# Moving the modulation sums of a two-layer trunk: new due places, each sum ordered behind a weight split, and a late set-up of the first norm

## The chip, the cores and the metric

One NeuronCore of a Trainium2 chip runs the whole program. The metric is device time in microseconds (us) of one launch. Before the change three runs took 1021.7, 1025.27 and 1025.34 us, a median of 1025.27.

## The reference, cut to what matters

The input is `x` of 256 rows by 1024 columns and a conditioning row `c` of 1024. Two layers have three sub-layers each: a SwiGLU mixer, a sequence mixer, a second SwiGLU mixer. Each sub-layer is modulated by three vectors of 1024 that come from `c`:

```
c_act = silu(c)
for l in range(2):
    mod = c_act @ mod_w[l] + mod_b[l]            # mod_w[l]: 1024 x 9216
    sh1, sc1, g1, sh2, sc2, g2, sh3, sc3, g3 = split(mod, 9)
    f = swiglu(x * (1 + sc1) + sh1, ffn_in[l, 0], ffn_out[l, 0])
    x = layer_norm(ALPHA * x + 0.5 * (1 + g1) * f, ln_g[l, 0], ln_b[l, 0])
    u = x * (1 + sc2) + sh2
    m = even_mixer(u) if l % 2 == 0 else odd_mixer(u)
    x = layer_norm(ALPHA * x + (1 + g2) * m, ...)
    ...                                          # third sub-layer: swiglu with sh3, sc3, g3
```

`swiglu(u) = (silu(u @ w_gate) * (u @ w_up)) @ w_out` with an inner width of 2816. All numbers are float32.

## The kernel before, in words

**Weights as one stream.** The activations stay on the chip with the 1024 columns on the partitions (8 tiles of 128 x 256). All weight matrices are laid out by the host in the order of use, as 170 slabs of 16 blocks of 128 x 128 (1 MiB each, tensor `wst`). `Stream.dma_to` issues the transfers on SyncE's queue (line 331) into the pool `wraw`, which has six buffers. `Stream.conv_to` turns each half slab (8 blocks, 128 x 1024) into two rounded parts: ScalarE writes `whi` (line 351), VectorE writes `wlo = raw - whi` (line 352). That pair is called a split here. `whi` and `wlo` have five buffers each, so splits can run at most five half slabs ahead of TensorE. `mm3` (lines 429 to 431) then makes three matmuls per block: hi by hi, hi by lo, lo by hi. A slab is thus 48 matmuls of 128 x 256. The first slab is used unsplit.

**Modulation sums.** `c_act @ mod_w` isn't done on TensorE. Its matrix is cut into 144 pieces of 128 x 1024; piece i gives the 128 numbers of one eighth of one of the 18 vectors. Two pieces make a 1 MiB transfer (tensor `modw`, line 386, also on SyncE's queue and in the same six `wraw` buffers); there are 72, called mods here, in the order of need: shift and scale of the first sub-layer side by side (mods 0 to 7), its gate (8 to 11), then shift (12 to 15) and scale (16 to 19) of the second, and so on. `Stream.reduce` multiplies a piece by `c_act` and adds along the row in one VectorE instruction (line 403, tile `junk`), then reads the accumulator. This is called a sum here; mod n holds sums 2n and 2n+1.

**What sets the order.** `MOD_TARGETS[s]` says how many mods must have been issued before weight slab s is. `dma_to(s)` first calls `mods_to(MOD_TARGETS[s])`, and a mod remembers the slab in front of which it was issued as its due slab. `conv_to` emits, after the split of a half slab, one sum if the oldest waiting one is due by that slab, and a second one if more than four are waiting. Transfers are issued about four slabs ahead of the split, so several mods wait at a time and sums mostly come out in pairs. `MOD_TARGETS` is made from `FIRST_MODS` (targets of the first slabs), `SHARE` (mods per sub-layer), `SKIP` and `ENDGAP` (slabs left free at a sub-layer's start and end). The first sub-layer is slabs 0 to 32: slabs 0 to 3 for the first half of the inputs and blocks j = 0 to 7 (`W.pause` keeps `conv_to` from emitting sums there), 4 to 11 for j = 8 to 15, 12 to 15 for the second half of j = 0 to 7 (whose earlier part sums lie in the tile `flat`, added at line 811), 16 to 21 for j = 16 to 21, and 22 to 32 for the output matrix. In `first_u` (up to line 567) each of the eight input tiles is modulated as soon as its own two sums are there.

The compiler's framework places the instructions of each engine in one fixed order at build time, from the order of emission, priorities (`tc.high_priority`) and its own picture of when operands are ready. `queue_behind(i, j)` only tells it that i must come after j on their engine. Each engine works through its list in order.

**The norm between sub-layers.** `Boundary(l, s, weight)` is made when the last matrix of a sub-layer begins. Its constructor fetches the gate with `W.mod` (line 583) and scale and shift of the next sub-layer (line 593). `W.mod` forces the transfers and emits all sums still missing for that vector at once. The constructor then makes small 128 x 8 columns `gate`, `A`, `B` and others (lines 585 to 604) and writes `A` and `B` as two extra columns of the tile `flat` (lines 610, 611). `tile_out(f, ps)` takes output tile f out of PSUM with `gate` (line 645) and prepares it for the next sub-layer with `A` (`scaled`, lines 617 and 618); `shift_out` does tile 0.

Of the kernel before, what the change touches and what calls it, by code (L numbers as in the profile page):

```python
# [12 lines left out]
F32R = mybir.dt.float32r  # L13
# [24 lines left out]
SLAB = 16  # L38
# [5 lines left out]
SH, SC, GT = 0, 1, 2  # L44
# [119 lines left out]
SUBS = []  # L164
# [47 lines left out]
def mod_targets():  # L212


    first = FIRST_MODS
    out, done = list(first), first[-1]
    for (a, b), n, skip in zip(SUBS, SHARE, SKIP):
        a, b = max(a // SLAB + skip, len(first)), b // SLAB - ENDGAP
        while len(out) < a:
            out.append(done)  # L220
        out += [done + int(math.ceil(n * (i + 1 - a) / (b - a))) for i in range(a, b)]
        done += n
    out += [NMODSLAB] * (NSLAB - len(out))
    return out


FIRST_MODS = (1, 2, 3, 4, 4, 4, 5, 5, 6, 7, 8, 8)
SHARE = (13, 11, 18, 18, 0, 4)
SKIP = (12, 14, 6, 6, 3, 8)
ENDGAP = 1  # L230
MOD_TARGETS = mod_targets()


@with_exitstack
def trunk_kernel(ctx: ExitStack, tc: tile.TileContext, xT, cvec, pos, wst, modw, colsd,
                 rgw, wa2, outT):
    nc = tc.nc
    sync, act, vec, pool, pe = nc.sync, nc.scalar, nc.vector, nc.gpsimd, nc.tensor
# [10 lines left out]
    wk = ctx.enter_context(tc.tile_pool(name="wk", bufs=2))  # L249
# [10 lines left out]
    def T(pl, shape, dt=F32, tag=None, **kw):  # L260
        return pl.tile(shape, dt, tag=tag, name=nm(tag), **kw)
# [42 lines left out]
    class Stream:  # L304
# [30 lines left out]
        def conv_to(self, n):  # L335

            self.dma_to((n - 1) // 2 + Stream.RAW)
            W2 = Stream.HS * P
            while self.nconv < min(n, 2 * NSLAB):
                s = self.nconv  # L340
                if s < 2 * RAWSLABS:

                    self.conv[s] = (self.raw[s // 2][:, (s % 2) * W2:(s % 2 + 1) * W2], None)
                    if s % 2:
                        self.raw.pop(s // 2)
                    self.nconv += 1
                    continue
                hi = T(whi, [P, W2], F32R, tag="whi")
                lo = T(wlo, [P, W2], F32R, tag="wlo")
                raw = self.raw[s // 2][:, (s % 2) * W2:(s % 2 + 1) * W2]  # L350
                ia = act.activation(hi, raw, AF.Copy)  # L351
                i = vec.tensor_tensor(lo, raw, hi.bitcast(F32), SUB)  # L352
                self.last_conv = ia, i
                if self.behind is not None:
                    queue_behind(i, self.behind)
                self.conv[s] = (hi, lo)
                if s % 2:
                    self.raw.pop(s // 2)
                self.nconv += 1
                if self.todo and not self.pause and self.todo[0][2] <= s // 2:  # L360
                    self.reduce()
                    if len(self.todo) > 4 and self.todo[0][2] <= s // 2:
                        self.reduce()

        def next(self, *keys):
            n = len(keys)
# [53 lines left out]
    W = Stream()  # L420
# [63 lines left out]
    def flat(q, dt=F32):  # L484

        return T(main, [P, KD * FROW], dt, tag=f"flat{q}")
# [88 lines left out]
    class Boundary:  # L575
        def __init__(self, l, s, weight):
            ta.use("abs_reciprocal_sqrt_and_small")
            self.next_table = "silu_and_others" if s != 0 else \
                "natural_log_exp_and_others" if l % 2 == 0 else "abs_reciprocal_sqrt_and_small"
            self.l, self.s, self.weight = l, s, weight  # L580
            self.values = None
            self.done = set()
            g = W.mod(l, 3 * s + GT)
            self.gate = T(wk, [P, KD], tag="gate")
            vec.tensor_scalar(self.gate, g, 1.0, weight, ADD, MULT)
            self.y = T(main, [P, KD, SEQ], tag="yy")
            self.acc = T(wk, [P, 2, SEQ], tag="acc", bufs=1)
            o = (l * 3 + s) * KD
            self.g, self.b = col("ln_g", o, KD), col("ln_b", o, KD)
            self.last = l == DEPTH - 1 and s == 2  # L590
            if not self.last:
                nl, ns = (l, s + 1) if s < 2 else (l + 1, 0)
                sc, sh = W.mod(nl, 3 * ns + SC), W.mod(nl, 3 * ns + SH)
                self.A = T(wk, [P, KD], tag="A")
                self.B = T(wk, [P, KD], tag="B")
                vec.scalar_tensor_tensor(self.A, sc, 1.0, self.g, ADD, MULT)
                vec.scalar_tensor_tensor(self.B, sc, 1.0, self.b, ADD, MULT)
                vec.tensor_tensor(self.B, self.B, sh, ADD)
                self.ag = T(wk, [P, KD], tag="ag")
                self.ab = T(wk, [P, KD], tag="ab")  # L600
                vec.tensor_scalar(self.ag, self.g, -0.5 * ALPHA, None, MULT)
                vec.tensor_scalar(self.ab, self.b, ALPHA, None, MULT)
                self.hA = T(wk, [P, KD], tag="hA")
                vec.tensor_scalar(self.hA, self.A, -0.5, None, MULT)

                self.next = (nl, ns)
                self.ya = [flat(q, F32R)[:, :KD * (SEQ + 2)].rearrange("p (k c) -> p k c", k=KD) for q in range(2)]
                hi, lo = self.ya
                for c, a in ((SEQ, self.A), (SEQ + 1, self.B)):
                    act.activation(hi[:, :, c], a, AF.Copy)  # L610
                    vec.tensor_tensor(lo[:, :, c], a, hi[:, :, c].bitcast(F32), SUB)

        def scaled(self, f):
            if not self.last:
                hi, lo = (t[:, f, :SEQ] for t in self.ya)
                y, a = self.y[:, f, :], self.A[:, f:f + 1]
                act.activation(hi, y, AF.Identity, scale=a)
                vec.scalar_tensor_tensor(lo, y, a, hi.bitcast(F32), MULT, SUB)  # L618
# [21 lines left out]
            self.p0 = (y, ysq)  # L640

        def tile_out(self, f, ps):
            y = self.y[:, f, :]
            with tc.high_priority():
                vec.scalar_tensor_tensor(y, ps, self.gate[:, f:f + 1], ax[:, f, :], MULT, ADD)  # L645
                if f == 0:
                    return
                ysq = T(wk, [P, SEQ], tag="ysq")
                act.activation(ysq, y, AF.Square)  # L649
                if f < KD - 1:  # L650
                    p = self.p0 if f == 1 else (self.acc[:, 0, :], self.acc[:, 1, :])
                    vec.tensor_tensor(self.acc[:, 0, :], p[0], y, ADD)
                    vec.tensor_tensor(self.acc[:, 1, :], p[1], ysq, ADD)  # L653
                self.scaled(f)
            if f == KD - 1:
                self.stats(y, ysq)
# [741 lines left out]
```

## Time and profile before

| what | value |
|---|---|
| median of 3 runs | 1025.27 us (1021.7 to 1025.34) |
| the profiled execution | 1021.95 us, of which the profile's span is 1020.2 us |
| TensorE matmul busy | 997.9 us, 98%, 8344 matmuls |
| VectorE busy | 877.1 us, 86% |
| ScalarE busy | 611.7 us, 60% |
| splits on VectorE (line 352) | 338, 1217 ns each |
| sums on VectorE (line 403) | 136 at 1275 ns and 8 more |
| granted TensorE clock | 0.996 |

PE in the profile is TensorE's matmuls, PEld its weight loads, DVE VectorE, ACT ScalarE, SP SyncE. In a timeline a row is start, duration, engine, line, operation, written tile <- read tiles, shapes; a bracket tells idle time of the engine before it and who ended it. In the rows of waits the numbers are us in total, times, and the longest. In the rows by window an engine's busy time stands with the count of its instructions, then the granted clock, the share of the transfer engines that was busy, and GB/s.

### The profile page before, as it was taken

To read this page: it belongs to the slowest core of one execution; us is meant where nothing else is said; L and a number is where in the kernel's file an instruction comes from. 1 tells how busy PE (TensorE), PEld (TensorE's weight loads), DVE (VectorE), ACT (ScalarE), POOL (GpSimd) and SP (SyncE) were. 2 spreads that over 40 slices of the span, in tenths; PEclk is the share of its full clock that TensorE was granted. 3 is DMA by queue.
4 is the path that set the end of the run, shared out by engine and by line. 5 is a ranking of instruction groups with operands and counts; after the bars stand their busy time and mean duration, and the time that the engine had idled before them with its cause. 6 is when DMAs were issued, how large, how long until landed. Compare 5 with 4: busy or idle time off the path is not lost.

```text
span 1020.2 us, 20536 instructions
## 1 busy us (share of the span) xinstructions
PE 997.9 (98%) x8344; PEld 977.2 (96%) x8344; DVE 877.1 (86%) x1503; ACT 611.7 (60%) x1021; POOL 6.7 (1%) x27
## 2 busy tenths in 40 slices
PE   9999999999999999999999999999999999999995
PEld 7999999998999999999999999999999899999995
DVE  5789999798999899999896899999788799666664
ACT  4756664578895666655545664454568777454542
POOL 0000000000000000000000000000000000000000
PEclk9999999999999999999999999999999999999998
DMA  9997798555468936799986469998743156766501
GB/s 345 416 378 294 284 351 322 218 206 177 155 247 314 351 123 211 280 380 368 358 298 244 160 260 379 328 332 333 282 165 125 48 176 240 266 227 244 191 17 42
DMA packets 38145, 258.56 MB, mean 253 GB/s; under 512 B 4241, under 2 KB 5777, under 8 KB 7714
## 3 DMA queue, kind: packets, MB, share of 16 engines
q1 hardware_dynamic: 38050, 257.25, 67.2%
q8 instruction: 65, 1.06, 0.4%
q14 instruction: 30, 0.25, 0.1%
HBM read 256.18 MB, written 1.05 MB: 252 GB/s over the span
## 4 chain that ended last, share of the span: by engine, by line
PE 84%; DVE 13%; issue 1%; ACT 1%; DVEq 0%; ACTq 0%
PE mm L430 24%; PE mm L429 24%; PE mm L431 24%; DVE wlo L352 4%; DVE junk L403 2%; PE mm L789 2%; PE mm L1068 1%; PE mm L1067 1%; PE mm L1069 1%; DVE yy L645 1%; DVE ax L633 1%; PE ax L789 1%; DVE flat L618 1%; DVE acc L653 0%; DVE flat L811 0%
## 5 line engine op out<-in xcount | busy, mean ns | idle before, releaser
L352 DVE TENSOR_TENSOR wlo<-wraw,whi 128x1024 fp32r<-128x1024 f32 x338 | 409.1, 1217 | 78.5 <-ACT whi L351 77.9
L351 ACT ACTIVATE whi<-wraw 128x1024 fp32r<-128x1024 f32 x338 | 355.4, 1058 | 187.0 <-PE mm L430 150.3
L429 PE MATMUL mm<-uhi,whi 128*128 128x256 f32 x1624 | 448.6, 278 | 2.7 <-ACT uhi L722 1.4
L430 PE MATMUL mm<-ulo,whi 128*128 128x256 f32 x1624 | 449.1, 277 | 0.4 <-DVE ulo L477 0.4
L431 PE MATMUL mm<-uhi,wlo 128*128 128x256 f32 x1624 | 448.8, 277 | 0.0
L429 PEld LDWEIGHTS mm<-uhi,whi 128*128 128x128 f32 x1624 | 304.1, 188 | 3.5 <-ACT uhi L722 1.6
L430 PEld LDWEIGHTS mm<-ulo,whi 128*128 128x128 f32 x1624 | 305.0, 188 | 0.9 <-DVE ulo L477 0.7
L431 PEld LDWEIGHTS mm<-uhi,wlo 128*128 128x128 f32 x1624 | 305.0, 188 | 0.1
L431 PE MATMUL mm<-hhi,wlo 128*128 128x256 f32 x704 | 194.8, 277 | 1.0 <-DVE wlo L352 1.0
L430 PE MATMUL mm<-hlo,whi 128*128 128x256 f32 x704 | 194.7, 277 | 0.0
L429 PE MATMUL mm<-hhi,whi 128*128 128x256 f32 x704 | 194.6, 276 | 0.0
L403 DVE CUSTOM_DVE_ANT_0 junk<-wraw,cact,cols 128x1024 bf16<-128x1024 f32 x136 | 173.3, 1275 | 7.4 <-DMA wraw<-modw 6.3
L431 PEld LDWEIGHTS mm<-hhi,wlo 128*128 128x128 f32 x704 | 132.2, 188 | 1.2 <-DVE wlo L352 1.2
L429 PEld LDWEIGHTS mm<-hhi,whi 128*128 128x128 f32 x704 | 132.2, 188 | 0.0
L430 PEld LDWEIGHTS mm<-hlo,whi 128*128 128x128 f32 x704 | 132.2, 188 | 0.0
L476 ACT ACTIVATE hhi<-h 128x256 fp32r<-128x256 f32 x88 | 35.7, 414 | 60.7 <-DVE h L766 60.5
L649 ACT ACTIVATE ysq<-yy 128x256 f32<-128x256 f32 x42 | 17.3, 414 | 41.9 <-DVE yy L645 39.1
L766 DVE SCALAR_TENSOR_TENSOR h<-mm,sg 128x256 f32<-128x256 f32 x75 | 30.5, 414 | 7.3 <-PE mm L431 7.0
L645 DVE SCALAR_TENSOR_TENSOR yy<-mm,gate,ax 128x256 f32<-128x256 f32 x48 | 23.0, 478 | 15.7 <-PE mm L431 15.7
L477 DVE TENSOR_TENSOR hlo<-h,hhi 128x256 fp32r<-128x256 f32 x88 | 35.6, 413 | 0.2 <-ACT hhi L476 0.2
L451 ACT ACTIVATE sg<-mm 128x256 f32<-128x256 f32 x75 | 27.4, 367 | 8.8 <-PE mm L431 4.9
L429 PE MATMUL mm<-flat,whi 128*128 128x258 f32 x96 | 28.7, 299 | 0.0
(310 smaller groups left out, 1112.1 us busy)
## 6 DMA issues: line engine op xcount, KB each, us to landing
wraw<-wst SPq DMA_DIRECT2D x165, 1024.0 KB, 6.2
wraw<-modw SPq DMA_DIRECT2D x71, 1024.0 KB, 7.2
wraw<-wst SPq DMA_DIRECT2D x10, 512.0 KB, 10.0
wraw<-modw SPq DMA_DIRECT2D x2, 512.0 KB, 5.1
yy<-xT SPq DMA_DIRECT2D x8, 128.0 KB, 10.2
wraw<-rgw SPq DMA_DIRECT2D x1, 1024.0 KB, 4.7
outT<-yy SPq DMA_DIRECT2D x3, 256.0 KB, 2.6
outT<-yy SPq DMA_DIRECT2D x2, 128.0 KB, 2.5
```

The source lines that it names most:

```text
L351: ia = act.activation(hi, raw, AF.Copy)
L352: i = vec.tensor_tensor(lo, raw, hi.bitcast(F32), SUB)
L403: i = vec.tensor_tensor_reduce(junk, t, cact, 1.0, bias, MULT, ADD, self.modcols[(l, v)][:, j:j + 1])
L429: pe.matmul(ps, hi, mh, start=start, stop=False, skip_group_check=shared)
L430: pe.matmul(ps, hi, ml, start=False, stop=False, skip_group_check=shared)
L431: pe.matmul(ps, lo, mh, start=False, stop=stop, skip_group_check=shared)
L451: i = act.activation(out, in_, func, **kw)
L476: act.activation(hi, src, AF.Copy)
L477: return vec.tensor_tensor(lo, src, hi.bitcast(F32), SUB)
L645: vec.scalar_tensor_tensor(y, ps, self.gate[:, f:f + 1], ax[:, f, :], MULT, ADD)
L766: vec.scalar_tensor_tensor(h, pu, bu, sg, ADD, MULT)
L789: pe.matmul(grp[j][:, half * SEQ:(half + 1) * SEQ], wt[w], mv, start=k == ks[0] and half == 0 and t == 0, stop=k == ks[-1] and t == len(te ...
```

## The change

The change has three parts. First, new due places for mods 4 to 20, in the first sub-layer: the targets for slabs 4 to 15 are now 4, 5, 6, 7, 8, 9, 10, 11, 12, 12, 12, 12 (before 4, 4, 5, 5, 6, 7, 8, 8, 9, 10, 10, 11), and the next nine mods go out in front of slabs 16 to 24, one each (before, the next ten were spread over slabs 16 to 30, and the set-up of the first norm asked for one of them early). From slab 30 on the targets are as before. Second, `conv_to` sets `self.after`, so that `reduce` orders each sum that it emits behind the split just emitted, on VectorE. The code does this for every sum that `conv_to` emits, in all sub-layers. Third, the first norm (layer 0, sub-layer 0) makes its gate when output tile 0 is taken out and `A`, `B` and the rest when tile 2 is, and then does `scaled` for tiles 0 and 1. The other norms do all of it in the constructor, through the new function `prepare`.

```
-    for (a, b), n, skip in zip(SUBS, SHARE, SKIP):
-        a, b = max(a // SLAB + skip, len(first)), b // SLAB - ENDGAP
+    for (a, b), n, skip, gap in zip(SUBS, SHARE, SKIP, ENDGAP):
+        a, b = max(a // SLAB + skip, len(first)), b // SLAB - gap
...
-FIRST_MODS = (1, 2, 3, 4, 4, 4, 5, 5, 6, 7, 8, 8)
-SHARE = (13, 11, 18, 18, 0, 4)
-SKIP = (12, 14, 6, 6, 3, 8)
-ENDGAP = 1
+FIRST_MODS = (1, 2, 3, 4, 4, 5, 6, 7, 8, 9, 10, 11, 12, 12, 12, 12)
+SHARE = (9, 11, 18, 18, 0, 4)
+SKIP = (16, 14, 6, 6, 3, 8)
+ENDGAP = (7, 1, 1, 1, 1, 1)
+
+LAZY = 2
...
                 if self.todo and not self.pause and self.todo[0][2] <= s // 2:
+
+                    self.after = i
                     self.reduce()
                     if len(self.todo) > 4 and self.todo[0][2] <= s // 2:
+                        self.after = i
                         self.reduce()
+                    self.after = None
...
-            g = W.mod(l, 3 * s + GT)
-            self.gate = T(wk, [P, KD], tag="gate")
-            vec.tensor_scalar(self.gate, g, 1.0, weight, ADD, MULT)
+            self.gate = None
+            self.lazy = LAZY if (l, s) == (0, 0) else -1
...
+            if self.lazy < 0:
+                self.prepare()
+
+        def prepare(self):
+            l, s = self.l, self.s
+            if self.gate is None:
+                g = W.mod(l, 3 * s + GT)
+                self.gate = T(wk, [P, KD], tag="gate")
+                vec.tensor_scalar(self.gate, g, 1.0, self.weight, ADD, MULT)
+            if self.lazy < 0 and not self.last:
+                nl, ns = self.next
                 sc, sh = W.mod(nl, 3 * ns + SC), W.mod(nl, 3 * ns + SH)
...
         def scaled(self, f):
-            if not self.last:
+            if not self.last and self.lazy < 0:
...
         def tile_out(self, f, ps):
+            if self.lazy >= 0:
+                if f == self.lazy:
+                    self.lazy = -1
+                self.prepare()
+                if self.lazy < 0:
+                    for q in range(f):
+                        self.scaled(q)
```

More of the change, by code (lines that the diff above doesn't have):

```diff
@@ L591, in __init__ @@
             if not self.last:
-                nl, ns = (l, s + 1) if s < 2 else (l + 1, 0)
+                self.next = (l, s + 1) if s < 2 else (l + 1, 0)
+                self.ya = [flat(q, F32R)[:, :KD * (SEQ + 2)].rearrange("p (k c) -> p k c", k=KD) for q in range(2)]
+            if self.lazy < 0:
[8 more added lines that the diff above has]
+                nl, ns = self.next
                 sc, sh = W.mod(nl, 3 * ns + SC), W.mod(nl, 3 * ns + SH)
@@ L604, in __init__ @@
                 vec.tensor_scalar(self.hA, self.A, -0.5, None, MULT)
-                self.next = (nl, ns)
-                self.ya = [flat(q, F32R)[:, :KD * (SEQ + 2)].rearrange("p (k c) -> p k c", k=KD) for q in range(2)]
                 hi, lo = self.ya
```

## The prediction

> **What bounds the kernel now.** I read the page's span and engines first.
>
> ```profile
> span 1020.2 us, 20536 instructions
> PE 997.9 (98%) x8344; PEld 977.2 (96%) x8344; DVE 877.1 (86%) x1503; ACT 611.7 (60%) x1021; POOL 6.7 (1%) x27
> ```
>
> TensorE is the bound: it is busy for 98% of the span. The change takes no matmul away, so it can only remove stretches in which TensorE waits, or add some. So the second view is the list of TensorE's waits, here from 12 us on.
>
> ```profile
> PE ax L1127 <- DVE ut L1129: 1.4, 1, 1.4
> PE mm L429 <- ACT uhi L722: 1.4, 1, 1.4
> PE mm L429 <- ACT sg L451: 1.3, 1, 1.3
> PE ax L1023 <- DVE la L1056: 1.1, 1, 1.1
> PE mm L431 <- DVE wlo L352: 1.0, 1, 1.0
> ```
>
> The change touches two of these, as the windows show: in the first sub-layer TensorE isn't full in 96 to 119 us (1.3 short) and, from the waits, once for a `wlo`.
>
> ```profile
> 40.00:60.00 20.00, 20.00 (x178) 20.00 (x178) 16.51 (x22) 10.44 (x16) 0.00 (x0) 1.00 1.02 415
> 60.00:80.00 20.00, 20.00 (x179) 20.00 (x178) 17.41 (x27) 10.59 (x20) 0.00 (x0) 1.00 0.91 352
> 80.00:96.00 16.00, 16.00 (x143) 15.98 (x142) 15.80 (x25) 9.39 (x14) 0.00 (x0) 1.00 0.68 251
> 96.00:119.00 23.00, 21.69 (x191) 21.49 (x191) 23.00 (x41) 14.19 (x25) 0.00 (x0) 1.00 0.80 302
> 119.00:133.00 14.00, 14.00 (x126) 14.00 (x125) 14.00 (x24) 9.17 (x16) 0.00 (x0) 1.00 0.81 307
> 133.00:160.00 27.00, 27.00 (x240) 27.00 (x240) 27.00 (x54) 15.52 (x20) 0.00 (x0) 1.00 0.93 351
> 160.00:197.00 37.00, 35.98 (x313) 35.59 (x313) 30.97 (x58) 19.44 (x28) 0.86 (x4) 1.00 0.76 285
> ```
>
> Three things stand here. 178 or 179 matmuls run in 20 us (some straddle an edge), so a slab of 48 takes about 5.4 us. VectorE (the fifth number) has 3.5 and 2.6 us to spare in 40 to 80, nothing from 96 to 160, and 6.0 us afterwards. The transfer engines (the last share) are full to beyond 60 us.
>
> Now the first stall, in VectorE's timeline and then in ScalarE's and TensorE's.
>
> ```profile
> 113.97 1.21 DVE L352 TENSOR_TENSOR wlo<-wraw,whi 128x1024 fp32r<-128x1024 f32 x1
> 115.11 1.27 DVE L403 CUSTOM_DVE_ANT_0 junk<-wraw,cact,cols 128x1024 bf16<-128x1024 f32 x1
> 116.31 0.07 DVE L403 DVE_READ_ACCUMULATOR2_ANT mod<- 128x1 f32 x1
> 116.31 0.41 DVE L477 TENSOR_TENSOR hlo<-h,hhi 128x256 fp32r<-128x256 f32 x1
> 116.65 0.67 DVE L811 TENSOR_TENSOR flat<-ax,flat 128x512 f32<-128x512 f32 x1
> 117.25 1.26 DVE L403 CUSTOM_DVE_ANT_0 junk<-wraw,cact,cols 128x1024 bf16<-128x1024 f32 x1
> 118.45 0.07 DVE L403 DVE_READ_ACCUMULATOR2_ANT mod<- 128x1 f32 x1
> 118.45 0.41 DVE L766 SCALAR_TENSOR_TENSOR h<-flat,sg 128x256 f32<-128x256 f32 x1
> 118.79 0.41 DVE L766 SCALAR_TENSOR_TENSOR h<-mm,sg 128x256 f32<-128x256 f32 x1
> 119.12 1.20 DVE L352 TENSOR_TENSOR wlo<-wraw,whi 128x1024 fp32r<-128x1024 f32 x1
> ```
>
> ```profile
> 117.42 0.42 ACT L451 ACTIVATE sg<-flat 128x256 f32<-128x256 f32 x1 [1.97 <-DVE flat L811]
> ```
>
> ```profile
> 118.16 0.39 PE L429 MATMUL mm<-uhi,whi 128*128 128x256 f32 x1 [1.31 <-ACT sg L451]
> ```
>
> TensorE needs a PSUM buffer back at 116.85. Its reader `sg` stands on ScalarE behind an `sg` that waited 1.97 us for the add at 116.65, and that add stood behind the sum at 115.11. From start to start a split costs VectorE 1.14 us, a sum about 1.2, an `hlo` or `h` 0.34, an add 0.60. The last split of the fence came after two sums of one mod (115.11 and 117.25). The second stall is in the output matrix.
>
> ```profile
> 157.32 1.21 DVE L352 TENSOR_TENSOR wlo<-wraw,whi 128x1024 fp32r<-128x1024 f32 x1
> 158.46 0.15 DVE L860 TENSOR_SCALAR rg_sp<-rg_sp 128x8 f32<-128x8 f32 x1
> 158.53 1.27 DVE L403 CUSTOM_DVE_ANT_0 junk<-wraw,cact,cols 128x1024 bf16<-128x1024 f32 x1
> ...
> 162.10 1.22 DVE L352 TENSOR_TENSOR wlo<-wraw,whi 128x1024 fp32r<-128x1024 f32 x1
> ```
>
> ```profile
> 163.38 0.39 PE L431 MATMUL mm<-hhi,wlo 128*128 128x256 f32 x1 [1.02 <-DVE wlo L352]
> ```
>
> The split at 162.10 comes late, behind the sums of mods 16 to 19. The constructor of the first norm emits these eight in one go, since they weren't due yet.
>
> **The change part by part.** The work itself stays: 144 sums, 338 splits, the same transfers, the same small columns. Only order and place move, so the terms are stalls that go and stalls that come. All due places below are worked out from the code's plan.
>
> *Slabs 4 to 15 (35 to 100 us).* Four more mods must pass by slab 12 (12 instead of 8). VectorE then has, per slab with a mod, two splits, two sums and for the last four input tiles one `ulo` (about an `hlo`): 2 x 1.14 + 2 x 1.2 + 0.34 = 5.0 us against 5.4 of TensorE. That fits, using the 6.1 us that 40 to 80 leaves free. The queue of transfers: a slab and a mod are 2.1 MB, at 415 GB/s 5.05 us, plus 0.3 us for an input tile of 0.13 MB, which is 5.4 of 5.4. It is full, but keeps pace. I put this at 0. Bounds: nothing below, since no matmul waits in 40 to 96 us now; above, a wait like the longest ones in the list, 1.4 us, twice.
>
> *Slabs 16 to 24 (100 to 150 us).* Up to 133 us the groups of VectorE's instructions from 96 us on say:
>
> ```profile
> L352 DVE TENSOR_TENSOR wlo<-wraw,whi 128x1024 fp32r<-128x1024 f32 x14 | 16.9, 1206 | 0.0
> L403 DVE CUSTOM_DVE_ANT_0 junk<-wraw,cact,cols 128x1024 bf16<-128x1024 f32 x8 | 10.2, 1270 | 0.0
> ```
>
> By the plan the sums of mods 8 to 11 are due three slabs (16 us) earlier than now and slabs 13 to 15 bring none, so I expect VectorE to reach 96 us about two splits and two sums ahead (2.3 + 2.4 = 4.7 us). The product steps of j = 0 to 7 (8 adds, 16 `h` and `hlo`: 4.8 + 5.4 = 10.2 us) and j = 16 (0.34) then share the engine with splits of slabs 17 and 18 (4 x 1.14 = 4.6) and sums 26 to 29 (4.8): 20 us, to 116.0. Before, the last of these steps began at 118.79. The 1.3 us stall asks for 1.3 us sooner; 2.8 are there. It goes: -1.3. Bounds: -1.3 and, if more sums are taken in between, the slower rival below.
>
> *The first norm.* Its columns cost the same as before. Mods 12 to 19 are now due by slab 23 at the latest and need no burst at slab 22, so no eight sums are emitted ahead of the splits; `A` is needed only at tile 2, some 22 us after the output matrix begins at about 133 us. What hides the columns and the late `scaled` of two tiles (0.4 us each on VectorE, by the 128x256 forms above) is VectorE's free 6.0 us in 160 to 197; without that cover they would cost 0.8 us. The stall of 1.0 goes: -1.0. Bounds -1.0 and 0.
>
> *All later sums.* The order behind a split holds for them too. The first sums of the second sub-layer move furthest, from an idle spot to behind a split 26 us later:
>
> ```profile
> 250.21 1.28 DVE L403 CUSTOM_DVE_ANT_0 junk<-wraw,cact,cols 128x1024 bf16<-128x1024 f32 x1 [0.64 <-DMA wraw<-modw]
> ...
> 276.60 1.21 DVE L352 TENSOR_TENSOR wlo<-wraw,whi 128x1024 fp32r<-128x1024 f32 x1
> ...
> 351.79 1.23 DVE L352 TENSOR_TENSOR wlo<-wraw,whi 128x1024 fp32r<-128x1024 f32 x1 [1.81 <-ACT whi L351]
> 353.94 2.36 DVE L352 TENSOR_TENSOR wlo<-wraw,whi 128x1024 fp32r<-128x1024 f32 x2 [0.92 <-ACT whi L351]
> ```
>
> Two sums are 2.4 to 2.6 us in a stretch where `la` holds TensorE up by 1.1 us already. They can push later work by at most 2.6; the idle 1.81 + 0.92 = 2.7 us near 352 take that up again before the transposes at L1127. I take 0, the end nearest those rows; bounds 0 and 2.6. What waits behind a sum that waits for its split: the next split on VectorE, and on SyncE's queue the transfer that reuses the sum's `wraw` buffer. In the later SwiGLU layers a split runs up to five half slabs (13 us) ahead of its use, so I price that at 0 as well.
>
> Sum: -1.3 - 1.0 = -2.3 us. The profiled execution took 1021.95 us (span 1020.2 and 1.75 around it) and would take 1019.65. The median of the three runs is 3.3 us above that execution. The forecast goes by the median: 1025.27 - 2.3 = 1023.0.
>
> **The rivals.**
>
> *It doesn't do what it says (0.30).* The condition for a second sum (more than four waiting) stays, and the plan gives pairs for nearly all of mods 4 to 18: "one by one" isn't what the code does. Pairs behind splits may hold the add just as now, and the stall at 118 us stays while only the one at 163 goes: -1.0, so 1024.3. For it: the pair in the fence was emitted after its splits already. Against it: VectorE's lead of 4.7 us.
>
> *Slower: VectorE falls behind in slabs 17 to 23 (0.13).* Due places put sums 26 to 39 behind splits up to slab 23, which are made before TensorE reaches 133 us. VectorE is full there now with 8 sums in 96 to 133; the lead covers sums up to 33. If the fixed order takes sums 34 to 39 ahead of the splits and product steps, 6 x 1.27 = 7.6 us come on top, and TensorE waits for `wlo` or PSUM. With the 1.0 saved later that is +6.6: 1031.9. It decides from the point where a split of slabs 20 to 23 ends after TensorE has come to it.
>
> *The transfers bind (0.06).* If the queue loses pace while mods 4 to 11 ride one per slab, every slab waits. The rows show 415 GB/s held in 40 to 60. At the 352 of 60 to 80 (where its share is down to 0.91) 2.1 MB take 6.0 us: 0.6 too many for seven slabs, +4.2, less 2.3: 1027.2. The Trainium skill, in "DMA: Bandwidth & Descriptors", section "Where 436 GB/s comes from", says that for transfers from HBM the HBM side, about 358 GB/s, binds. By that rule this rival's number is about what would come; the 415 GB/s of this trace speak against the rule here.
>
> *More goes than I count (0.08).* If the shifted sums also free `la`, `ut` and `uhi`, all five stalls of the list go: 6.2 us, 1019.1; from the fastest run, 1021.7, 1015.5. Against it: these three waits are in the second sub-layer and behind its norm, where targets don't move.
>
> **How the numbers follow.** The forecast has 0.43. About 0.5% (5.1 us) is what a measurement of this kernel can tell from no change. Forecast, first rival, most of the transfers rival and a part of the last lie within it: 0.80. Slower by more: the second rival at most of its price and the far end of the third, 0.13. Faster by more: only the last rival together with the spread of runs, 0.07. The range takes in the full price of the slower rival half way and the runs' own spread of 3.6 us below the median: from 1023.0 down to 1018.0 (-2.3 from the fastest run is 1019.4, and part of the last rival), up to 1030.5.
>
> **What would show it.** Right: in the waits of TensorE the rows for `sg` and for `wlo` are gone, windows 96 to 119 and 160 to 197 show PE full up to the norm, VectorE has idle time already before 160 us, and transfers stay full to about 72 us. The step on slabs 16 to 24 is wrong if TensorE still waits there for `sg`, or newly for `wlo`. The step on later sums is wrong if new waits stand between 270 and 400 us. The forecast as a whole is wrong if the median leaves 1018 to 1030.5.

## The result, and the profile after

| | runs | median, us | lowest to highest |
|---|---|---|---|
| before | 6 | 1022.51 | 1021.7 to 1025.34 |
| after | 6 | 1032.32 | 1030.94 to 1035.64 |

The ratio is 1.0102, with a 95% interval of 1.0088 to 1.0115. The change makes the kernel 9.8 us slower, and the median lies above the range of the prediction. The profiled execution took 1035.32 us, one of the longer of the six.

First the page's span and engines, for the kernel after.

```profile
span 1033.6 us, 20527 instructions
PE 1005.1 (97%) x8344; PEld 981.4 (95%) x8344; DVE 878.6 (85%) x1503; ACT 614.8 (59%) x1021; POOL 6.7 (1%) x27
```

The same 8344 matmuls, and the work of VectorE and ScalarE is the same to 0.5%. So the 13.4 us of span are not work: by the slab starts below some 9.7 are waits, and about 3.4 come with two stretches of half clock (last section). TensorE's waits from 12 us on, the longest:

```profile
PE ax L1149 <- DVE ut L1151: 3.0, 1, 3.0
PE mm L437 <- DVE wlo L354: 3.0, 6, 1.0
PE mm L435 <- ACT whi L353: 2.0, 3, 0.9
PE mm L435 <- ACT uhi L744: 1.4, 1, 1.4
...
PE ax L643 <- ACT shift L641: 0.6, 1, 0.6
...
PE mm L435 <- ACT sg L457: 0.2, 1, 0.2
```

The wait for `sg` has shrunk to 0.2 as forecast. In its place stand three waits for `whi`, which means ScalarE, an engine that the prediction never priced; six for `wlo`; and the wait at the transposes (L1149, which was L1127) has gone from 1.4 to 3.0. The windows show where:

```profile
40.00:60.00 20.00, 18.87 (x162) 18.43 (x161) 14.94 (x21) 9.59 (x14) 0.00 (x0) 1.00 0.97 382
60.00:80.00 20.00, 19.09 (x164) 18.73 (x163) 16.54 (x24) 7.78 (x11) 0.00 (x0) 1.00 0.86 334
80.00:96.00 16.00, 14.44 (x114) 13.33 (x114) 16.00 (x28) 12.23 (x22) 0.00 (x0) 1.00 0.85 311
96.00:119.00 23.00, 23.00 (x205) 23.00 (x205) 23.00 (x39) 13.16 (x21) 0.00 (x0) 1.00 0.86 313
119.00:133.00 14.00, 12.77 (x109) 12.38 (x109) 14.00 (x25) 7.49 (x15) 0.00 (x0) 1.00 0.76 295
133.00:160.00 27.00, 26.17 (x227) 25.77 (x227) 25.50 (x43) 16.36 (x21) 0.00 (x0) 1.00 0.93 355
160.00:197.00 37.00, 36.37 (x321) 36.18 (x320) 30.34 (x63) 18.76 (x27) 0.00 (x0) 1.00 0.66 242
```

Read the counts here, not the busy times. In 40 to 96 us TensorE ran 162 + 164 + 114 = 440 matmuls, before 178 + 179 + 143 = 500. Sixty matmuls at 20 / 178.5 = 0.112 us are 6.7 us. The busy times show a lack of only 3.6: in the timeline a matmul's row lasts 0.28 us although the rows start 0.11 us apart, so the row ahead of a wait covers its first part, and the matmul behind a wait is drawn longer (0.39). The rows of waits are too short for the same reason. So two thirds of the loss lie in the stretch that the prediction called free, and 96 to 119 us is full, as it said.

To follow the loss through the program and through all kernels, I took from each trace the start of a slab's first weight load and subtracted the same in before. Where a stretch of half TensorE clock (last section) lies ahead of the slab, half its length is taken out. In before, slab 4 starts at 34.8 us, 9 at 62.1, 16 at 100.3, 21 at 129.1, 25 at 151.0, 26 at 156.4, 28 at 168.6, 54 at 335.6, 59 at 367.9 and 140 at 846.3. The lags in us, for after and for the experiments below:

| kernel | 4 | 9 | 16 | 21 | 25 | 26 | 28 | 54 | 59 | 140 |
|---|---|---|---|---|---|---|---|---|---|---|
| after | 0.5 | 3.8 | 7.2 | 7.8 | 8.9 | 9.8 | 8.5 | 8.4 | 9.7 | 9.7 |
| places alone | -0.7 | 4.4 | 6.1 | 5.6 | 6.0 | 8.6 | 7.4 | 7.4 | 7.5 | 7.5 |
| order alone | 0.0 | 0.0 | 0.0 | 2.1 | 2.1 | 4.0 | 2.8 | 2.7 | 3.9 | 3.8 |
| set-up alone | 0.2 | 0.2 | 0.2 | 0.2 | 1.5 | 1.5 | 0.2 | 0.2 | -0.3 | 0.0 |
| no order | 0.1 | 5.2 | 6.9 | 6.4 | 6.9 | 7.2 | 5.9 | 5.8 | 5.9 | 6.0 |
| old early places | 0.5 | 0.5 | 0.5 | 5.5 | 7.8 | 7.8 | 6.5 | 6.3 | 7.7 | 7.7 |
| modulation held back | 0.1 | 1.4 | 1.9 | 2.4 | 3.8 | 3.8 | 2.5 | 2.6 | 2.5 | 2.5 |
| before, held back | 1.2 | 1.2 | 1.2 | 1.2 | 1.2 | 1.2 | 1.3 | 1.2 | 1.1 | 1.2 |
| single sums | 0.0 | 3.4 | 6.8 | 6.5 | 6.5 | 7.9 | 6.7 | 6.9 | 8.4 | 8.9 |
| no order, held back | 0.3 | 0.3 | 0.8 | 0.1 | 0.2 | 0.2 | -1.1 | -1.2 | -1.2 | -1.2 |
| set-up, gate early | -0.5 | -0.5 | -0.5 | -0.5 | -0.5 | -0.5 | -1.8 | -1.8 | -1.8 | -1.5 |
| late places, held back | -0.6 | -0.6 | -0.6 | 2.0 | 2.5 | 3.7 | 2.4 | 2.4 | 2.4 | 2.5 |
| order in the first sub-layer | -0.1 | 3.4 | 6.8 | 7.3 | 7.6 | 7.8 | 6.5 | 6.5 | 6.5 | 6.4 |
| no order, held back, gate early | 0.1 | 0.3 | 0.8 | 0.1 | 0.2 | 0.2 | -1.1 | -1.2 | -1.2 | -1.2 |

Only differences along a row count (the first column is the start). In after 6.7 us come between slabs 4 and 16, 1.3 net between 16 and 28 (2.6 up to slab 26, less the 1.3 of before's wait at 163 us, which is gone), and 1.3 between 54 and 59. After slab 59 nothing moves until the end.

The first 6.7 us are to be seen on ScalarE. First its waits in 35 to 96 us of after, then, in 35 to 80 us, of before.

```profile
ACT uhi L560 <- DVE mod L409: 14.3, 4, 3.9
```

```profile
ACT uhi L554 <- DVE mod L403: 13.3, 4, 4.1
```

Four times, once for each of the input tiles 4 to 7, ScalarE stands for some 3.5 us in front of the modulation of a tile (`uhi`, then `ut`), which needs both sums of that tile's mod. Before has this wait too. What differs is what is queued behind it. ScalarE's timeline, after and then before:

```profile
43.13 0.60 ACT L560 ACTIVATE uhi<-yy,mod,mod 128x256 fp32r<-128x256 f32 x1 [3.25 <-DVE mod L409]
...
44.13 1.99 ACT L353 ACTIVATE whi<-wraw 128x1024 fp32r<-128x1024 f32 x2
...
50.02 0.60 ACT L560 ACTIVATE uhi<-yy,mod,mod 128x256 fp32r<-128x256 f32 x1 [3.59 <-DVE mod L409]
...
51.02 1.99 ACT L353 ACTIVATE whi<-wraw 128x1024 fp32r<-128x1024 f32 x2
...
57.90 1.99 ACT L353 ACTIVATE whi<-wraw 128x1024 fp32r<-128x1024 f32 x2
...
64.78 1.99 ACT L353 ACTIVATE whi<-wraw 128x1024 fp32r<-128x1024 f32 x2
```

```profile
42.47 0.60 ACT L554 ACTIVATE uhi<-yy,mod,mod 128x256 fp32r<-128x256 f32 x1 [1.75 <-DVE mod L403]
...
43.47 2.00 ACT L351 ACTIVATE whi<-wraw 128x1024 fp32r<-128x1024 f32 x2
...
50.88 2.00 ACT L351 ACTIVATE whi<-wraw 128x1024 fp32r<-128x1024 f32 x2
```

The clock times are nearly the same; the slab isn't. Counted from the first split, the `whi` at 44.13 in after are those of slab 6, the `whi` at 43.47 in before those of slab 7. With the slab starts of TensorE beside them (of the same traces), the lead being the time from the first `whi` to TensorE's start of the slab:

| tile | before: slab, `whi` starts, TensorE at the slab | lead | after: slab, `whi`, TensorE | lead |
|---|---|---|---|---|
| 4 | 7: 43.47, 51.17 | 7.7 | 6: 44.13, 46.21 | 2.1 |
| 5 | 8: 50.88, 56.61 | 5.7 | 7: 51.02, 52.11 | 1.1 |
| 6 | 9: 57.89, 62.05 | 4.2 | 8: 57.90, 58.99 | 1.1 |
| 7 | 10: 64.90, 67.49 | 2.6 | 9: 64.78, 65.87 | 1.1 |

Each step is one round. In after it is both `whi` of a slab, the first `wlo`, a sum, the second `wlo`, a sum, `uhi`, then the next slab's `whi`; in before both sums stand behind the second `wlo`. In after a round takes 6.88 us (44.13, 51.02, 57.90, 64.78), in before 7.0 to 7.4, against 5.44 us in which TensorE uses a slab up. Each round thus loses 1.4 to 2 us of lead. Before enters with 7.7 and comes out with 2.6. After enters with 2.1 and is down to 1.1 a round later, which is no lead: one `whi` takes about 1.05 us, and TensorE starts the slab as it ends, so that the next two slabs take TensorE 6.88 us each as well. Neither VectorE nor ScalarE is full in this loop (14.9 and 9.6 of the 20 us from 40 on).

The rounds themselves cost 3.3 of the 6.7 us (up to slab 9). The rest follows by slab 14: VectorE did 31.5 us of work from 40 to 80, in before 33.9, though more sums were due. From 80 to 96 it is full with what is left, and TensorE waits for `wlo` and `h`.

The Trainium skill, in "PSUM — Partial Sum Buffer", section "Engine vs sequencer instructions", says that the queues of ScalarE and VectorE are strictly first in, first out; the trace agrees, with each `whi` of the fence for after starting right behind a `uhi` and `ut` that had waited 3.25 to 3.89 us.

### The profile page after: what moved, and what is told of

The parts are those of the page before. It is cut to its first block, busy times and chain, and to the rows that moved or that the text cites. A ratio compares the mean times of both kernels' runs of the same rounds, so it can differ in the third digit from the quotient of the medians.

```text
span 1033.6 us, 20527 instructions
## 1 busy us (share of the span) xinstructions
PE 1005.1 (97%) x8344; PEld 981.4 (95%) x8344; DVE 878.6 (85%) x1503; ACT 614.8 (59%) x1021; POOL 6.7 (1%) x27
## 3 DMA queue, kind: packets, MB, share of 16 engines
HBM read 256.18 MB, written 1.05 MB: 249 GB/s over the span
## 4 chain that ended last, share of the span: by engine, by line
PE 80%; DVE 14%; issue 3%; ACT 2%; DMA 1%; SPq 0%; DVEq 0%; ACTq 0%
PE mm L436 23%; PE mm L437 23%; PE mm L435 23%; DVE wlo L354 5%; DVE junk L409 3%; PE mm L811 2%; ACT whi L353 1%; PE mm L1089 1%; PE mm L1090 1%; PE mm L1091 1%; DMA wraw<-wst 1%; DVE h L788 1%; PE ax L811 1%; DVE hlo L483 1%; DVE flat L633 0%
## 5 line engine op out<-in xcount | busy, mean ns | idle before, releaser
L483 DVE TENSOR_TENSOR hlo<-h,hhi 128x256 fp32r<-128x256 f32 x88 | 36.9, 427 | 0.5 <-ACT hhi L482 0.5
```

The lines of the kernel that those rows point to most:

```text
L483: return vec.tensor_tensor(lo, src, hi.bitcast(F32), SUB)
```

## The experiments

**The three parts alone.** Before with the new places (`FIRST_MODS`, `SHARE`, `SKIP`, `ENDGAP`) and nothing else:

```
-FIRST_MODS = (1, 2, 3, 4, 4, 4, 5, 5, 6, 7, 8, 8)
+FIRST_MODS = (1, 2, 3, 4, 4, 5, 6, 7, 8, 9, 10, 11, 12, 12, 12, 12)
...
```

> The kernel before with the new due places alone. Theory 1 (the places cost, through ScalarE's order): in this build the modulation of input tile 4, which waits for both sums of mod 4, stands on ScalarE in front of the splits of slab 5, where it stands in front of slab 7 in the kernel before and of slab 6 in the changed one. The round of sums, modulation, split takes about 6.9 us per slab against 5.4 of TensorE, so the lead is used up sooner: at slab 16 TensorE is 7 us or more behind the kernel before, in all +7 to +11 us. Theory 2 (the order behind the splits costs): without that order the time stays within 2 us of the kernel before. Theory 3 (transfers bind): about +4 us, with ScalarE's splits waiting for weights rather than for sums.

Measured: 1030.74 us against 1022.3, ratio 1.0081 (1.0066 to 1.0096). This part alone makes most of the loss, 6.8 us of it before slab 16. In this kernel the modulation of tile 4 stands in front of slab 5's split, one slab earlier than in after. TensorE's waits in 35 to 200 us are two rows, and both are waits for splits:

```profile
PE mm L429 <- ACT whi L351: 4.1, 5, 1.2
PE mm L431 <- DVE wlo L352: 3.5, 3, 2.5
```

Before with the order behind the splits alone:

```
+                    self.after = i
                     self.reduce()
                     if len(self.todo) > 4 and self.todo[0][2] <= s // 2:
+                        self.after = i
                         self.reduce()
+                    self.after = None
```

> The kernel before with only the order of each sum behind its split. Theory 1: the modulation of input tile 4 stands in front of slab 8 or 7 as before, so slabs 5 to 16 lose nothing: within 2 us of the kernel before, plus up to 1.5 us of a longer wait before the transposes in the second sub-layer. Theory 2: most of the loss is here, +7 to +10 us. Theory 3: within 2 us.

Measured: 1028.33 us, ratio 1.0054 (1.0037 to 1.0071). The 6.0 us lie between theory 1 (3.5 at most) and theory 2 (7 to 10). Nothing is lost up to slab 16, as theory 1 said; then 4.0 us by slab 26, which it didn't have, and 1.2 at slabs 54 to 59. TensorE's timeline has these waits up to 122 us, and a third of 1.68 us for a `wlo` at 158.21:

```profile
115.89 0.39 PE L435 MATMUL mm<-uhi,wlo 128*128 128x256 f32 x1 [1.04 <-DVE wlo L352]
120.28 0.39 PE L433 MATMUL mm<-uhi,whi 128*128 128x256 f32 x1 [1.61 <-ACT sg L455]
```

The second is before's wait for `sg`, at the same place and longer: there was 1.3. So the order makes the stall that the change was expected to remove a little worse. It also holds sums back into the product steps: the last sum of the gate begins at 100.36 us, in before at 94.98.

Before with the late set-up of the first norm alone:

> The kernel before with only the late set-up of the first norm. All theories: the one wait for wlo in the output matrix (1.0 us) may go: between -1.5 and +0.5 us.

Measured: 1022.66 us, ratio 1.0001 (0.9991 to 1.0011). The lags show two things that cancel: 1.3 us lost by slab 25, and 1.3 gained by slab 28, where before waited for a `wlo`. The loss, in VectorE's timeline:

```profile
147.20 0.17 DVE L604 TENSOR_SCALAR gate<-mod 128x8 f32<-128x8 f32 x1
147.27 1.22 DVE L354 TENSOR_TENSOR wlo<-wraw,whi 128x1024 fp32r<-128x1024 f32 x1
148.41 0.48 DVE L663 SCALAR_TENSOR_TENSOR yy<-mm,gate,ax 128x256 f32<-128x256 f32 x1
```

The first output tile is taken out at 148.41, in before at 143.34, because the gate stands 9 us later on VectorE. The rows of before:

```profile
138.25 0.15 DVE L585 TENSOR_SCALAR gate<-mod 128x8 f32<-128x8 f32 x1
...
143.34 0.48 DVE L645 SCALAR_TENSOR_TENSOR yy<-mm,gate,ax 128x256 f32<-128x256 f32 x1
```

ScalarE's `shift` reads that tile, and a matmul waits 1.0 us for it. The three parts alone cost 8.4, 6.0 and 0.4 us, together 9.8. They don't add up, so each is also taken away from after.

**Taking one part away.** After without the order:

```
-                    self.after = i
                     self.reduce()
...
```

> The changed kernel without the order behind the splits (new places and late set-up stay). Theory 1: like the new places alone, +6 to +11 us against the kernel before. Theory 2: the loss goes, within 2 us of the kernel before or faster. Theory 3: about +4 us.

Measured: 1028.3 us, ratio 1.0056 (1.0041 to 1.0071). The early loss stays (6.8), the later ones go: slabs 16 to 28 gain 1.0, and at slab 59 nothing happens. In this kernel too the modulation of tile 4 stands one slab earlier still, in front of slab 5's split (38.64 us).

After with before's places for slabs 4 to 15 (ten mods left for slabs 16 to 24):

```
-FIRST_MODS = (1, 2, 3, 4, 4, 5, 6, 7, 8, 9, 10, 11, 12, 12, 12, 12)
-SHARE = (9, 11, 18, 18, 0, 4)
+FIRST_MODS = (1, 2, 3, 4, 4, 4, 5, 5, 6, 7, 8, 8, 9, 10, 10, 11)
+SHARE = (10, 11, 18, 18, 0, 4)
```

> The changed kernel with the due places of slabs 0 to 15 as in the kernel before (11 mods by slab 15); slabs 16 to 24 bring the next ten, order and late set-up stay. Theory 1: the early round begins where it did before, so slabs 5 to 16 lose nothing and what is left of the loss is at most 3 us (slabs 24 to 26 and the wait before the transposes). Theory 2: the loss of 10 us stays. Theory 3: most of the loss goes, as in theory 1, but the waits for weights in slabs 16 to 24 grow.

Measured: 1029.98 us against 1022.29, ratio 1.0073 (1.0056 to 1.0090). Before slab 16 nothing is lost now: the early places are the cause of the 6.7 us. But 7.2 us appear between slabs 16 and 25, so that 7.7 are left where theory 1 allowed 3. About 2.0 of them stand at slab 25, where a matmul waits 1.7 us for `shift`; the gate is made at 153.03 here. The new early places do take load off VectorE, as the prediction said; the price is paid earlier.

**Is it ScalarE's queue?** After with the modulation of tiles 4 to 7 ordered on ScalarE behind the first `whi` of the slab four further on (slab 8 for tile 4), that is, about two slabs later. The sums, splits and transfers keep their order:

```
                 self.last_conv = ia, i
+                self.acts[s] = ia
...
             on_act.append(act.activation(uhi[:, k, :], x0[:, k, :], AF.Identity, bias=sh0[:, kk], scale=scp0[:, kk]))
+            if not stepwise:
+                queue_behind(on_act[-1], W.acts[2 * k + 8])
...
         on_act.append(act.activation(ut, x0[:, k, :], AF.Identity, bias=sh0[:, kk], scale=scp0[:, kk]))
+        if not stepwise:
+            queue_behind(on_act[-1], on_act[-2])
```

> The changed kernel; the modulation of input tiles 4 to 7 is ordered on ScalarE behind the first split of the slab that uses it (tile k behind slab k+4), so no split waits for sums there. Theory 1: the 6.9 us round is cut; slabs 5 to 12 run at 5.4 us and 4 to 7 of the 10 us go. If instead VectorE or the buffers of raw weights set the pace, less than 2 us go.

Measured: 1028.57 us, ratio 1.0059 (1.0044 to 1.0074). Of the 6.7 us up to slab 16 only 1.8 are left. By the medians 3.5 of the 9.8 us go, less than the 4 to 7 expected; by the spans of the two profiled executions (1033.6 and 1026.2) it is 7.4. The medians mix in stretches of half clock (last section). The windows to 96 us:

```profile
40.00:60.00 20.00, 18.97 (x167) 18.77 (x166) 18.66 (x26) 10.30 (x14) 0.00 (x0) 1.00 1.02 418
60.00:80.00 20.00, 20.00 (x179) 20.00 (x178) 18.22 (x29) 11.33 (x20) 0.00 (x0) 1.00 1.01 419
80.00:96.00 16.00, 15.96 (x138) 15.63 (x137) 15.48 (x24) 10.13 (x18) 0.00 (x0) 1.00 0.79 300
```

484 matmuls instead of 440. VectorE does more in 40 to 80 than in after (36.9 us instead of 31.5), with the same sums, because its splits no longer wait for a ScalarE that waits for its sums. Most of what is left, 1.3 of the 1.8 us, is one wait in 40 to 60 that the edit brings itself: tile 4 comes late for slab 8.

```profile
58.85 0.39 PE L438 MATMUL mm<-ulo,whi 128*128 128x256 f32 x1 [1.03 <-DVE ulo L572]
```

The same edit in before:

> The kernel before with the same order for the modulation of input tiles 4 to 7. Theory 1: its lead at slab 10 is larger, TensorE had no wait there, so the time changes only by what the later backlog of VectorE gains: between -2 and 0 us. If the place of the modulation itself is critical, it is slower by 1 to 3 us.

Measured: 1022.17 us, ratio 1.0000 (0.9991 to 1.0010). So holding the modulation back is no gain in itself; it only undoes what the new places did.

Both together, after without the order and with the modulation held back:

> The changed kernel without the order behind the splits, and with the modulation of input tiles 4 to 7 behind the first split of the slab that uses it. Two separate causes are claimed: the places through ScalarE's order in slabs 5 to 16 (6.8 us, of which this order gave back 4.8), and the order behind splits in slabs 16 to 28 and before the transposes (2 to 5 us and 1.3 us). If they are separate and these two edits undo them, the time is within 2 us of the kernel before: 1021 to 1024.5. If the places cost by the transfers or the buffers of raw weights as well, it stays at 1026 or above.

Measured: 1021.14 us against 1022.43, ratio 0.9989 (0.9980 to 0.9998). The new places now cost 0.5 us to slab 16:

```profile
40.00:60.00 20.00, 20.00 (x179) 20.00 (x178) 19.46 (x26) 10.39 (x14) 0.00 (x0) 1.00 1.02 417
60.00:80.00 20.00, 20.00 (x179) 20.00 (x179) 17.73 (x29) 11.29 (x19) 0.00 (x0) 1.00 1.01 421
80.00:96.00 16.00, 15.88 (x138) 15.57 (x137) 15.96 (x24) 10.15 (x18) 0.00 (x0) 1.00 0.92 360
```

It also settles the transfers: the same ones run at 417 and 421 GB/s for 40 us with TensorE full. The 382 and 334 of after are not their limit; SyncE's queue waits there 39 of the 40 us for VectorE to free a buffer.

**Is it the pairs?** After with pairs of sums only if more than twelve wait:

```
-                    if len(self.todo) > 4 and self.todo[0][2] <= s // 2:
+                    if len(self.todo) > 12 and self.todo[0][2] <= s // 2:
```

> The changed kernel with one sum at most behind a split (the second one is never emitted in practice). Theory 1: ScalarE's order is the same, so the early loss stays: within 2 us of the changed kernel. Rival: the pairs are what delays the splits; then 4 us or more of the 10 go.

Measured: 1033.78 us, ratio 1.0111 (1.0095 to 1.0126). Nothing changes up to slab 16 (6.8 lost), but nothing could: VectorE's instructions stand in the same order in both kernels up to 110 us, because in after the sums come one by one there already, each behind its own split. So this run can't tell what pairs cost early. The kernel without the order can: its sums come in pairs there, and it loses the same 6.8. Behind slab 16 single sums lose 1.4 us less to slab 28 and 0.7 more from 54 to 140. My first rival, that the code keeps its pairs, is true of the code but, up to slab 16, not of the engine.

**The gate.** Set-up alone as above, but with the gate made in the constructor and only `A`, `B` at tile 2:

> The kernel before with A and B of the first norm made at their first use, but the gate in the constructor, as before. Theory: late set-up alone gained nothing since the late gate holds tile 0 and its shift matmul (1.0 to 1.3 us wait) where a wait for wlo went (1.0 us). With the early gate both are gone: 1.0 to 1.5 us faster than the kernel before. Rival: the wait for wlo had moved for another reason; then no difference.

Measured: 1021.03 us against 1022.43, ratio 0.9987 (0.9978 to 0.9996). The loss at slab 25 is gone and the gain at slab 28 stays: 1.3 us. The gate stands at 137.75 here, and tile 0 is taken out at 142.73. The two changes of the set-up must be told apart: late `A`, `B` gain, a late gate loses as much.

**Late places.** No order, modulation held back, gate early, but before's places to slab 15 and ten mods in slabs 16 to 24:

> The places of slabs 0 to 15 as before, the next ten mods in front of slabs 16 to 24, no order behind splits, A and B late with an early gate, the modulation of tiles 4 to 7 behind the first split of the slab that uses it. Theory: no early round, no late order; what is left are the waits at slab 19 (1.3 us) and in the output matrix, and the places there take sums out of the output matrix: 0 to 2.5 us faster than the kernel before. Rival (more sums in slabs 16 to 24 overload VectorE there by themselves): 1 to 4 us slower.

Measured: 1025.15 us against 1022.43, ratio 1.0026 (1.0015 to 1.0037); 4.3 us lost between slabs 16 and 26 with no order at all: the rival was right. So ten mods in that stretch cost even without the order. Nine mods there cost nothing net where the new early places had taken sums away before (no order, held back: 0.8 at slab 16, 0.2 at slab 26).

**The transposes.** After with the order for the first sub-layer's sums only:

```
-                    self.after = i
+                    self.after = i if s < 66 else None
...
```

> The changed kernel with the order behind splits for the sums of the first sub-layer alone. Theory: the 1.3 us before the transposes of the second sub-layer come from the order of its own sums: 1 to 1.5 us of the 10 go, the rest stays. Rival: they come from the first sub-layer being late; then nothing goes.

Measured: 1029.03 us against 1022.43, ratio 1.0063 (1.0050 to 1.0077). Slabs 54 to 59 lose nothing, and TensorE's wait is back at before's size:

```profile
PE ax L1149 <- DVE ut L1151: 1.4, 1, 1.4
```

In after VectorE's timeline at this place reads

```profile
361.49 0.17 DVE L614 SCALAR_TENSOR_TENSOR A<-mod,cols 128x8 f32<-128x8 f32 x1
...
366.71 1.23 DVE L354 TENSOR_TENSOR wlo<-wraw,whi 128x1024 fp32r<-128x1024 f32 x1 [1.90 <-ACT whi L353]
367.85 0.87 DVE L1151 SCALAR_TENSOR_TENSOR ut<-ax,cols,yy 128x256 f32<-128x256 f32 x2
```

and in before

```profile
347.93 0.15 DVE L596 SCALAR_TENSOR_TENSOR A<-mod,cols 128x8 f32<-128x8 f32 x1
```

The `ut` for which TensorE waits 3.0 us stands behind a split that waits 1.90 us for its `whi`; before has such a wait too (1.81). What is later is the head of the chain, the column `A` of this norm, which needs the last sums. ScalarE's next instruction waits for it (3.06 us in before), and the `whi` come behind that. In before `A` is made at 347.93; with the lag of 8.4 and 1.7 for the clock that would be 358.0 in after, and it is 361.49, because each of the last sums stands behind a split. The idle time that I had counted as a reserve comes after `A` on the chain, so it moves along instead of taking anything up.

**Both gains at once.** No order, modulation held back, and the gate in the constructor:

> This kernel keeps the new places, sets no order behind splits, holds ScalarE's modulation of tiles 4 to 7 behind the first split of the slab four further on, and makes the gate of the first norm in its constructor (A and B at tile 2). Theory: the places cost nothing once the modulation no longer stands in front of the next splits, and the late gate is the only part of the set-up that costs; the two gains (0.9989 for the kernel with the late gate, and 1.3 us at slabs 26 to 28 where the gate came first with the old places) are in different stretches and add up: 0.9976, 2.4 us below before, with no TensorE wait for wlo or shift between 119 and 165 us. Rival: with the new places the late gate costs nothing, since VectorE has time there; then it equals 0.9989, 1.1 us below before, and the wait for the shift is absent in both or present in both.

Measured: 1021.54 us against 1022.13, ratio 0.9993 (0.9984 to 1.0002). The two gains don't add up: the early gate adds nothing here, and the lags are those of the kernel with the late gate. The rival forecast that, but not for its reason. VectorE's timeline says why. With the gate written in the constructor the row is

```profile
75.74 0.16 DVE L609 TENSOR_SCALAR gate<-mod 128x8 f32<-128x8 f32 x1
```

and with the gate written at its first use

```profile
75.74 0.16 DVE L610 TENSOR_SCALAR gate<-mod 128x8 f32<-128x8 f32 x1
```

It stands at the same time in both, 68 us ahead of its use. The instructions of TensorE, VectorE and ScalarE stand in the same order in both kernels from start to end, so this run doesn't test the gate; 0.9989 and 0.9993 are two measurements of one order. In after the gate is made at 98.60. The program's builder can thus place it far ahead of where the code emits it, and "made at its first use" is then not what happens on the engine. What decides the place isn't shown: early sums alone don't, for with the modulation held back and the order kept the last sum of the gate begins at 83.26 (in after 88.92) and the gate stands at 151.21.

## Why the prediction was wrong

**The step that failed: "Slabs 4 to 15 ... I put this at 0".** It measured 6.7 us. (All in all the miss is 12.1 us: against the 1022.51 of six runs the forecast of -2.3 means 1020.2. The 1025.27 of three runs was a high base.) I counted VectorE (5.0 us a slab) and the transfers (5.4) against TensorE's 5.4, each for itself, and both counts held: after the modulation is held back and the order taken off, the same sums and transfers run beside a TensorE that loses 0.5 us. What I left out is that the sums have a reader on ScalarE, `uhi`, and that ScalarE works in a fixed order with splits behind it. Moving the sums of mods 4 to 7 one or two slabs earlier moved `uhi` one slab earlier in that order, in front of a split with 2.1 us of lead instead of 7.7, and that is one round's loss away from waiting. The clue was in the trace of before: four waits of ScalarE for `mod`, 13.3 us in all, which harm nobody there. I looked only at TensorE's waits. My upper bound, "a wait like the longest ones in the list, 1.4 us, twice", priced a single wait, not a loop that comes round four times. How the loss divides is shown: 4.9 us go with the place of `uhi` alone. Of the other 1.8, 1.3 are the wait for `ulo` of tile 4 that the held-back modulation brings, and it goes when the order goes too (0.5 is left). With before's early places the order costs nothing there.

**"Slabs 16 to 24": -1.3.** Half right. The wait for `sg` is down to 0.2 and 96 to 119 us is full. But new waits stand right behind, mostly for `wlo`: 1.2 us are missing in 119 to 133, 0.8 in 133 to 160. "Newly for `wlo`" was this step's own sign of being wrong. By the slab starts after gains 1.1 at slab 19 and then loses 3.7 up to slab 26. Without the order, with the same places, 1.6 are gained and 1.8 lost, so about half of the new waits come from the order and the rest from the places. Part of them is another queue, the wait of 0.6 for `shift`. ScalarE's timeline of after:

```profile
153.57 1.06 ACT L353 ACTIVATE whi<-wraw 128x1024 fp32r<-128x1024 f32 x1 [4.37 <-DMA wraw<-wst]
154.54 0.40 ACT L641 ACTIVATE shift<-yy 128x256 fp32r<-128x256 f32 x1
```

The `shift` stands behind a split that waits 4.37 us for its weights, which are needed later than it.

**"The first norm": -1.0.** The wait at 163 us is gone, worth 1.3. The prediction put it down to the eight sums; between the two splits at 157.32 and 162.10 stand one sum and about 2.4 us of `A`, `B`, the output tile and other small work. In the kernel with before's places the late gate took the same 1.3 back, a term that I didn't have. I asked what hides the late columns, not who reads the gate. In after the gate isn't late at all.

**"All later sums": 0, bounds 0 and 2.6.** It measured 1.3 in slabs 54 to 59, with the wait for `ut` up from 1.4 to 3.0. I let the idle 2.7 us near 352 absorb it; that idle time stands behind the late column on the very chain that TensorE waits for.

**The rivals.** The slower one, 1031.9, comes within 0.5 us of the result for the wrong reason: it put 7.6 us into slabs 17 to 23, where 0.8 net were lost. Its mechanism exists, as the kernel with before's early places shows (5.2 us from slab 16 to 23), but after had moved that load away. The transfers don't bind. By the Trainium skill, "DMA: Bandwidth & Descriptors", section "Where 436 GB/s comes from", the HBM side would hold them at about 358 GB/s, which the section works out as half of what a stack gives two cores. This program runs on one core, and its windows with 417 and 421 GB/s disagree. Pairs instead of single sums change nothing up to slab 16.

**What was right:** no work is added, the -1.3 and the -1.0 are there to be had, and the order is not needed for either. With both harms taken out the kernel runs about 0.1% faster than before (0.9989 and 0.9993; the second interval reaches no change), 0.6 to 1.3 us of the 2.3 that I had counted. By the slab starts the two stalls give 1.6 and 1.3 back; a new wait for a `wlo` at 121 us takes 1.0 (its row shows 0.7), and 0.5 is lost ahead of slab 16.

## What to carry to other kernels

Before moving a step earlier, ask who reads its result, on which in-order engine that reader stands, and what is queued behind it: a consumer that waits harmlessly today is carried along in front of something that has no lead. Two engines that wait for each other in turn make a loop. Compare its period with the bound engine's, and its number of rounds with the lead at its start; busy shares don't show it. And look where an instruction really stands in the engine's timeline before pricing the place at which the code emits it, or trusting a run that moves it.

## What was not expected of the hardware

The granted TensorE clock falls to a half for stretches of 3.4 us. The windows around two of them in after:

```profile
237.00:241.00 4.00, 4.00 (x11) 2.95 (x10) 3.12 (x6) 2.84 (x5) 0.00 (x0) 0.57 0.23 92
...
370.00:374.00 4.00, 3.67 (x19) 3.53 (x18) 3.23 (x10) 1.23 (x3) 0.00 (x0) 0.59 0.96 365
```

Each costs about 1.7 us, half its length: with that taken out the rows of the table run on level. The profile of before has none until its last 10 us, where every kernel here runs at half clock. They come at the same points of the program: with the lag taken out, near 229 us in four of the fifteen profiles, within 357 to 361 in six, and once elsewhere. The second place is the restart of TensorE around the transposes. All five kernels with the order in the second sub-layer have a stretch there (in one it lasts 6.8 us), and of the ten others one. That fits with the times of those five, which lie 0.5 to 3.9 us above what their rows say (the last column less the first), against 0.7 at most for the others, so a part of the order's price may be clock. No run changes the clock alone.

The Trainium skill, in "TensorE: Matmul & The Clock Gate", section "Part 1: The HAM clock gate (the "warmup" mystery)", says that the clock falls to a half after an idle window of about 3.4 us and comes back after a busy one. The length of 3.4 us and the factor agree. The idle time doesn't: the longest wait ahead of the stretch at 370.7 is 3.0 us, in the kernel with the set-up alone it is 1.5, and ahead of the one at 237.6 the list of TensorE's waits in after has none from 200 us on. What these places have in common is few matmuls in the 7 us before, here in the kernel with the set-up alone:

```profile
352.00:359.00 7.00, 5.08 (x41) 4.48 (x40) 6.08 (x9) 4.91 (x8) 0.00 (x0) 1.00 0.96 377
359.00:362.50 3.50, 3.50 (x18) 3.50 (x18) 2.76 (x8) 1.36 (x4) 0.00 (x0) 0.51 0.97 372
```

41, where a full 7 us holds 62. That isn't enough either: before has as few at the same place, and keeps its clock.

```profile
352.00:359.00 7.00, 5.10 (x42) 4.50 (x41) 6.08 (x9) 4.73 (x8) 0.00 (x0) 1.00 1.00 394
```

What triggers a stretch wasn't tried.
